# Two gatings cut in two parts and placed in the last projection of an SSD layer, and its first norm placed one chunk later

## The chip, the cores and the metric

The kernel runs on one core of one Trainium2 chip. The metric is the time of one execution on the device in microseconds (us). All times are of that core; the profile of the kernel before was taken in one further execution.

## The reference, cut to what matters

The program computes one inference step of a two-layer decoder trunk for a prompt of 1024 rows and 8 sample rows, 1032 in all (T), at a width of 1024. Layer 0 joins an SSD branch (16 heads) and a convolution branch; both are gated, laid side by side and projected back to the width. Then come the residual and a layer norm. Layer 1 is sparse attention. The change is in the end of layer 0:

```python
y = y.reshape(b, l, SSD_INNER) * jax.nn.silu(z_a)               # gate of the SSD branch
y = y.reshape(b, l, SSD_GROUPS, SSD_INNER // SSD_GROUPS)        # 2 groups of 512 channels
y = y * lax.rsqrt(jnp.mean(jnp.square(y), -1, keepdims=True) + EPS)
y_a = y.reshape(b, l, SSD_INNER) * norm_g
...
out = jnp.concatenate([y_a, y_b], axis=-1) @ w_out              # w_out: 2048 x 1024
x_new = layer_norm(ALPHA * x + out, ln_g, ln_b)
```

## The kernel before, in words

Channels lie on the 128 partitions and rows along the free dimension, so a width of 1024 is 8 tiles of 128 x 1032. Rows are worked on in three chunks of 344: `CH = [(0, 344), (344, 344), (688, 344)]`; below they are the first, second and third chunk. Products keep float32 accuracy by splitting each operand in a high and a low part; `mm3` makes three matrix products for each tile of 128 input channels (lines 132 to 134). One output tile of 128 channels over one chunk is thus 8 x 3 = 24 products, and a chunk of the whole projection is 8 x 24 = 192.

The SSD branch leaves its heads in `xs[0..7]`. Channel tiles 4 to 7 are group 1, tiles 0 to 3 are group 0. `gate(g, t0, n)` does one group on one chunk: for each of its four tiles a load of the saved SiLU of z (`dza`, line 707), a multiplication on VectorE (line 708), a square on ScalarE (line 709) and, from the second tile on, an addition to the running sum (line 711). A product with a matrix of 1/512 (line 714) sums over the partitions; it is f32 and shows as two instructions. ScalarE makes 1/sqrt of it in two steps (lines 174 and 175), each with its table load, and VectorE scales the four tiles (line 718). Four of the six gatings stand among the eight tiles `out_b(m)` of the other branch's projection. The last two, group 0 on the second and third chunk, stand later, before the last projection.

`halves` splits `xs` into the high and low parts `ya` that the projection reads (line 778 on ScalarE, 779 on VectorE or GpSimd). `weights(h, ms)` loads half h of the weights of output tile m (line 763), casts the high part (764) and subtracts for the low part (765, odd m on GpSimd). `rows` loads a chunk's partial results (line 800) into the tiles `part`: two pools, `parts0` for the first and third chunk and `parts1` for the second.

The last loop runs over the three chunks. In the first, the upper four input tiles (kts 4 to 7) of output tiles m = 0 to 6 come first, 12 products each, then the lower four, with the tile added to `part` by line 825; m = 7 is last. The later chunks do 24 products for each m and add by line 830. The results stand in PSUM, in tiles of tag `pp` (two buffers; even m in the later chunks) or `pt` (five buffers, odd m). Behind each chunk stands `layer_norm`: a sum over the eight tiles (line 844), two products for the mean (846 and 847), the subtraction (851), squares (853) and their sum (857), a product for the variance (861), 1/sqrt (174 and 175), scaling (867), the parts for the next layer (868 and 869), the shift (870) and two stores to `dx1` (line 832), issued on GpSimd's queue. The tiles p and q of the norm are of tag `pt`.

The order on each engine is not the order of the program. The build puts the instructions in order by a simulated clock (`schedule_with_timeline_sim=True`): of those that are ready by that clock, the one that stands first in the program goes first. At run time each engine works its queue strictly in that order. Tiles of one tag share the tag's buffers, and the pools `gz`, `ob` and the heads' pool `ssd` give their place to later pools; here `parts1` lies where `gz` lay.

Of the kernel before, what the change touches and what calls it, by code (L numbers as in the profile page):

```python
# [9 lines left out]
F32 = mybir.dt.float32  # L10
# [8 lines left out]
T = 1032  # L19
NP = 1024  # L20
NS = 8
CH = [(0, 344), (344, 344), (688, 344)]
# [62 lines left out]
def psum(k, shape, tag, bufs, dt=F32):  # L85
    return k.t(k.ps, shape, dt, tag, bufs)


def pp(k):
    return psum(k, [128, 344], "pp", 2)  # L90


def pt(k):
    return k.t(k.pb, [128, 512], F32, "pt", 5)


def pm(k):
    return psum(k, [128, 512], "pm", 1)
# [19 lines left out]
def wk(w, kt, m=128, halves=2):  # L118
    per = 8 // halves
    hi, lo = w[kt // per]  # L120
    o = (kt % per) * m
    return hi[:, o : o + m], lo[:, o : o + m]


def mm3(k, out, w, act, t0, n, m=128, halves=2, kts=range(8), start=True, stop=True):

    nc = k.nc
    for kt in kts:
        wh, wl = wk(w, kt, m, halves)
        ah, al = act[kt]  # L130
        ah, al = ah[:, t0 : t0 + n], al[:, t0 : t0 + n]
        nc.tensor.matmul(out, wh, ah, start=(start and kt == kts[0]), stop=False)  # L132
        nc.tensor.matmul(out, wh, al, start=False, stop=False)  # L133
        last = nc.tensor.matmul(out, wl, ah, start=False, stop=(stop and kt == kts[-1]))  # L134
    return last.ins
# [35 lines left out]
def rstd_chunk(k, out, var):  # L171

    nc = k.nc
    nc.scalar.activation(out, var, AF.Ln, bias=k.epsb, scale=1.0)
    nc.scalar.activation(out, out, AF.Exp, scale=-0.5)


def layer0(k):
    nc, A, tc, ctx = k.nc, k.A, k.tc, k.ctx
# [202 lines left out]
    for t0, n in CH:  # L382
        p = pt(k)[:, :n]
# [11 lines left out]
    for t0, n in CH:  # L395
        p = pt(k)[:, :n]
# [75 lines left out]
    gzp = ob_es.enter_context(k.pool("gz"))  # L472
# [6 lines left out]
    for t0, n in CH:  # L479
        p = pp(k)  # L480
        mm_stacked(k, p[:32, :], wdt, x, t0, n)
        nc.scalar.activation(dtr[:32, t0 : t0 + n], p[:32, :], AF.Identity, bias=c("dtb")[:32], scale=1.0)
    p = pm(k)
# [28 lines left out]
    p = pm(k)  # L512
# [13 lines left out]
    for hf in range(2):  # L526
        p = pm(k)
# [3 lines left out]
        sl = slice(hf * 512, hf * 512 + 512)  # L531
# [3 lines left out]
    p = pm(k)  # L535
# [4 lines left out]
    p = pm(k)  # L540
    for hh in range(8):
        for q in range(2):
            h = 2 * hh + q
# [154 lines left out]
    nc.sync.dma_start(A["ssdconv_p"], scp)  # L698


    def gate(g, t0, n):
        sl = slice(t0, t0 + n)
        ob = lambda: k.t(gzp, [128, 344], F32, "gz", 7)
        sm = None
        for i in range(4 * g, 4 * g + 4):
            z = ob()
            nc.sync.dma_start(z, dza[i][:, sl])
            nc.vector.tensor_tensor(xs[i][:, sl], xs[i][:, sl], z, op=ALU.mult)
            nc.scalar.activation(z, xs[i][:, sl], AF.Square)
            if sm is not None:  # L710
                nc.vector.tensor_tensor(z, z, sm, op=ALU.add)
            sm = z
        p = pm(k)[:, :n]
        nc.tensor.matmul(p, k.ones["o512"], sm, start=True, stop=True)
        rs = ob()
        rstd_chunk(k, rs, p)
        for i in range(4 * g, 4 * g + 4):
            nc.vector.scalar_tensor_tensor(xs[i][:, sl], xs[i][:, sl], c("ng")[:, i : i + 1], rs, op0=ALU.mult, op1=ALU.mult)
# [9 lines left out]
    def out_b(m):  # L728
        w = load_w(k, A["W"][OB + m], eng=nc.gpsimd)
        ps = []  # L730
        if m == 7:
            ps = [pp(k), pp(k), pt(k)[:, :344]]
            for p, (t0, n) in zip(ps, CH):
                mm3(k, p, w, yb, t0, n, kts=range(4), stop=False)
        for t0, n in CH:
            o = k.t(obp, [128, 344], F32, "ob", 4)
            nc.sync.dma_start(o, A["xT"][:, m, t0 : t0 + n])
            p = ps.pop(0) if ps else pp(k)
            mm = mm3(k, p, w, yb, t0, n, kts=range(4 * (m == 7), 8), start=m < 7)
            if t0 == 344:  # L740
                four_pages(mm)
            nc.vector.scalar_tensor_tensor(o, o, ALPHA, p, op0=ALU.mult, op1=ALU.add)
            nc.sync.dma_start(dpart[m][:, t0 : t0 + n], o)

    for m in range(8):
        out_b(m)
        if 1 <= m <= 4:
            gate(1 - (m - 1) // 3, *CH[(m - 1) % 3])

# [5 lines left out]
    def weights(h, ms):  # L757
        for m in ms:
# [14 lines left out]
    ya = {i: (k.t(yh_pool, [128, T], F32R, "yh", 8), k.t(*((yh_pool, [128, T], F32R, "yl", 4) if i > 3 else (Yb, [128, T], F32R, "yb", 4))))  # L773
          for i in (4, 5, 6, 7, 0, 1, 2, 3)}

    def halves(i, t0, n):
        sl = slice(t0, t0 + n)
        nc.scalar.copy(ya[i][0][:, sl], xs[i][:, sl])
        (nc.gpsimd if t0 and i % 2 else nc.vector).tensor_tensor(
            ya[i][1][:, sl], xs[i][:, sl], ya[i][0][:, sl].bitcast(F32), op=ALU.subtract)  # L780

    for i in range(4, 8):
        halves(i, *CH[0])
    for t0, n in CH[1:]:
        gate(0, t0, n)
    for i in range(4, 8):
        halves(i, 344, T - 344)
    for i in range(4):
# [2 lines left out]
    op = es.enter_context(k.pool("outp0"))  # L791
    parts = [es.enter_context(k.pool(f"parts{j}")) for j in range(2)]

    dx1 = k.t(dram, [8, 128, T], F32, "dx1")

    def rows(sl):

        prs = [k.t(parts[sl.start == 344], [128, 4, 344], F32, "part", 2) for _ in range(2)]
        for h, pr in enumerate(prs):
            nc.sync.dma_start(pr, dpart[4 * h : 4 * h + 4, :, sl].rearrange("m p t -> p m t"))  # L800
        return prs

    prs = rows(slice(0, 344))
    weights(0, range(8))
    weights(1, range(2))


    for t0, n in CH:
        sl = slice(t0, t0 + n)
        if t0:  # L810
            prs = rows(sl)
            for i in range(4):
                halves(i, t0, n)
        part = [prs[m // 4][:, m % 4, :] for m in range(8)]
        if t0 == 0:
            ps = []
            for m in range(8):
                p = pt(k)[:, :n] if m in (1, 3, 4, 5, 6) else pp(k)
                mm3(k, p, [None, first[m]] if m < 2 else W[m], ya, t0, n, kts=(4, 5, 6, 7), stop=False)
                ps.append(p)  # L820
                if m < 6:
                    continue
                for j in range(7) if m == 6 else (7,):
                    mm3(k, ps[j], W[j], ya, t0, n, kts=(0, 1, 2, 3), start=False)
                    nc.vector.tensor_tensor(part[j], part[j], ps[j], op=ALU.add)
        else:
            for m in range(8):
                p = pt(k)[:, :n] if m % 2 else pp(k)
                mm3(k, p, W[m], ya, t0, n)
                nc.vector.tensor_tensor(part[m], part[m], p, op=ALU.add)  # L830
        layer_norm(k, op, part, n, t0 + n == T, lambda m: [a[:, sl] for a in ya[m]],
                   lambda h, prs=prs, sl=sl: nc.gpsimd.dma_start(dx1[4 * h : 4 * h + 4, :, sl].rearrange("m p t -> p m t"), prs[h]))
    es.close()
    r1_es.close()
    k.x1 = ya
# [3 lines left out]
def layer_norm(k, pool, z, n, last, hl, store):  # L839

    nc, c = k.nc, k.c
    s = k.t(pool, [128, 344], F32, "sum", 1)[:, :n]
    for m in range(1, 7):
        nc.vector.tensor_tensor(s, s if m > 1 else z[0], z[m], op=ALU.add)
    p = pt(k)[:, :n]
    nc.tensor.matmul(p, k.ones["o1024"], s, start=True, stop=False)
    nc.tensor.matmul(p, k.ones["o1024"], z[7], start=False, stop=True)
    q = pt(k)[:, :n]
    sm = None
    for m in range(8):  # L850
        nc.vector.tensor_tensor(z[m], z[m], p, op=ALU.subtract)
        sq = k.t(pool, [128, 344], F32, "sq", 3)[:, :n]
        nc.scalar.activation(sq, z[m], AF.Square)
        if last:
            nc.tensor.matmul(q, k.ones["o1024"], sq, start=(m == 0), stop=(m == 7))
        elif m:
            nc.vector.tensor_tensor(sm, sm, sq, op=ALU.add)
        else:
            sm = sq
    if not last:  # L860
        nc.tensor.matmul(q, k.ones["o1024"], sm, start=True, stop=True)
    rs = k.t(pool, [128, 344], F32, "rs", 1)[:, :n]
    rstd_chunk(k, rs, q)
    for m in range(8):
        hi, lo = hl(m)
        g, b = c("lng")[:, m : m + 1], c("lnb")[:, m : m + 1]
        nc.vector.scalar_tensor_tensor(z[m], z[m], g, rs, op0=ALU.mult, op1=ALU.mult)
        nc.scalar.activation(hi, z[m], AF.Identity, bias=b, scale=1.0)
        nc.vector.scalar_tensor_tensor(lo, z[m], b, hi.bitcast(F32), op0=ALU.add, op1=ALU.subtract)
        nc.gpsimd.tensor_scalar(z[m], z[m], b, 1.0, op0=ALU.add, op1=ALU.mult)  # L870
        if m % 4 == 3:
            store(m // 4)
# [1033 lines left out]
def build(tc, A):  # L1906
    with ExitStack() as ctx:
        k = K(tc, A, ctx)
        setup(k)
        layer0(k)  # L1910
        layer1(k)
# [22 lines left out]
```

## Time and profile before

| what | value |
|---|---|
| time before, median of 3 runs | 1652.54 us (1650.47 to 1658.17) |
| the profiled execution | 1655.23 us, its span 1653.4 us |
| mean granted TensorE clock | 0.986 |
| TensorE (PE) busy | 1582.2 us, 96% |
| VectorE (DVE) busy | 1147.5 us, 69% |
| ScalarE (ACT) busy | 863.9 us, 52% |
| GpSimd (POOL) busy | 424.9 us, 26% |
| last projection, first chunk | 797.69 to 834.10 us of the span |
| second chunk | 834.10 to 873.73 us |
| third chunk | 873.73 to 906.04 us |

A row of the trace's timeline begins with the start and the duration in us, then the engine, the line of the kernel and the operation with its output and inputs by tile name; the bracket at its end is the time for which the engine stood idle before and what ended it. Busy times of PE overlap from one instruction to the next; starts are what counts. PEclk is the TensorE clock that was granted, 1.00 being full speed. The engines' queues are in order, SyncE's (SPq, which issues nearly all loads) too.

### The profile page before, as it was taken

The page shows a single profiled execution, that of the slowest core. Times are in us where ns is not written, and L with a number is a line of the kernel's source. Part 1 is how long each engine was busy: PE and PEld are TensorE (multiplying, and loading weights), DVE is VectorE, ACT ScalarE, POOL GpSimd, SP SyncE. Part 2 cuts the span into 40 slices and gives each one's busy share as a digit, 9 for nine tenths or more (in the row PEclk, how much of TensorE's full clock was granted, in tenths as well). Part 3 has the DMA queues.
Part 4 walks back from the last instruction along what each step waited for, and adds up shares of the span by engine and source line. Part 5 has one row for each costly group of instructions (what it writes and reads, how often), then busy time and mean ns, then how long its engine had stood idle before and what let it go on. Part 6 is the DMA issues. An engine that isn't in the chain of part 4 may idle for free. (4 is left out here: it accounts for less than half of the span.)

```text
span 1653.4 us, 28870 instructions
## 1 busy us (share of the span) xinstructions
PE 1582.2 (96%) x10374; PEld 1426.8 (86%) x10374; DVE 1147.5 (69%) x2375; ACT 863.9 (52%) x1959; POOL 424.9 (26%) x752
## 2 busy tenths in 40 slices
PE   7999989989999998999989999999999899999997
PEld 7999989989999997899889899989997577666675
DVE  4788977542356778684867555999998766565674
ACT  5255433562345556353542544578854855556673
POOL 4000000001222224122514301168762511123330
PEclk9999989999999999999999999999999999999999
DMA  7332232336111145443523321132455413322231
GB/s 231 118 111 73 72 102 95 133 122 216 56 33 52 67 135 177 143 130 97 163 89 106 100 87 39 63 106 92 145 168 172 119 45 109 97 76 63 65 94 45
DMA packets 147397, 173.66 MB, mean 105 GB/s; under 512 B 20117, under 2 KB 111597, under 8 KB 146997
## 3 DMA queue, kind: packets, MB, share of 16 engines
q1 hardware_dynamic: 144596, 165.80, 31.9%
q0 software_dynamic: 1216, 4.37, 0.8%
q10 hardware_dynamic: 1440, 1.65, 0.4%
q8 instruction: 81, 1.33, 0.3%
q14 instruction: 64, 0.52, 0.1%
HBM read 124.04 MB, written 49.82 MB: 105 GB/s over the span
## 5 line engine op out<-in xcount | busy, mean ns | idle before, releaser
L132 PE MATMUL pp<-act,whi 128*128 128x344 f32 x1008 | 328.0, 327 | 13.6 <-ACT act L233 8.1
L134 PE MATMUL pp<-act,wlo 128*128 128x344 f32 x1008 | 329.0, 328 | 10.7 <-DVE wlo L109 10.7
L133 PE MATMUL pp<-act,whi 128*128 128x344 f32 x1008 | 328.0, 325 | 0.9 <-POOL act L726 0.8
L132 PEld LDWEIGHTS pp<-act,whi 128*128 128x128 f32 x1008 | 192.8, 192 | 17.2 <-ACT act L233 8.1
L134 PEld LDWEIGHTS pp<-act,wlo 128*128 128x128 f32 x1008 | 193.1, 192 | 13.1 <-DVE wlo L109 11.6
L133 PEld LDWEIGHTS pp<-act,whi 128*128 128x128 f32 x1008 | 193.1, 192 | 3.3 <-POOL act L726 1.1
L109 POOL TENSOR_TENSOR wlo<-wst,whi 128x512 fp32r<-128x512 f32 x86 | 116.6, 1357 | 305.0 <-ACT whi L108 262.1
L108 ACT CAST whi<-wst 128x512 fp32r<-128x512 f32 x150 | 92.2, 618 | 154.2 <-PE pp L133 74.5
L334 DVE SCALAR_TENSOR_TENSOR uv<-uv,cst,uv 128x1024 f32<-128x1024 f32 x120 | 157.8, 1315 | 2.6
L132 PE MATMUL pp<-yh,whi 128*128 128x344 f32 x412 | 132.9, 323 | 1.5 <-ACT ev L1196 1.5
L134 PE MATMUL pp<-yh,wlo 128*128 128x344 f32 x412 | 132.6, 322 | 1.3 <-POOL wlo L109 1.2
L1510 DVE CUSTOM_DVE_ANT_0 P<-lg,w 128x512 f32<-128x512 f32 (+3 forms) x144 | 82.9, 597 | 55.2 <-PE lg L1509 49.8
L1509 PE MATMUL lg<-w,Q 128*128 128x512 f32 (+3 forms) x384 | 102.4, 371 | 6.3 <-DVE nmx L1510 6.0
L1536 PEld LDWEIGHTS tr<-cst,P 128*128 128x128 f32 x576 | 64.6, 141 | 29.0 <-issue 17.8
L1536 PE MATMUL tr<-cst,P 128*128 128x128 f32 x576 | 85.2, 281 | 4.1 <-ACT P L1514 3.4
L109 DVE TENSOR_TENSOR wlo<-wst,whi 128x512 fp32r<-128x512 f32 x64 | 43.8, 692 | 63.6 <-ACT whi L108 63.2
L1509 PEld LDWEIGHTS lg<-w,Q 128*128 128x128 f32 x384 | 62.8, 191 | 25.6 <-DVE nmx L1510 13.3
L1545 PE MATMUL pv<-ph,V 128*64 128x256 f32 (+1 forms) x640 | 82.6, 375 | 2.0 <-DVE ph L1539 0.9
L134 PEld LDWEIGHTS pp<-yh,wlo 128*128 128x128 f32 x412 | 77.4, 188 | 3.9 <-POOL wlo L109 2.4
L132 PEld LDWEIGHTS pp<-yh,whi 128*128 128x128 f32 x412 | 77.4, 188 | 3.7 <-ACT ev L1196 1.8
L1514 ACT ACTIVATE P<-P,mx 128x1024 f32<-128x1024 f32 (+3 forms) x64 | 63.3, 989 | 30.1 <-DVE mx L1513 27.2
L351 ACT ACTIVATE cft<-cw,own 128x80 f32<-128x80 f32 x256 | 66.2, 349 | 20.8 <-PE pt L353 12.2
(634 smaller groups left out, 4023.3 us busy)
## 6 DMA issues: line engine op xcount, KB each, us to landing
wst<-in_W SPq DMA_DIRECT2D x166, 256.0 KB, 2.9
qst<-dq SPq DMA_DIRECT2D x64, 128.0 KB, 2.8
q<-in_ck SPq DMA_DIRECT2D x64, 128.0 KB, 2.3
vp<-in_cv SPq DMA_DIRECT2D x64, 128.0 KB, 2.1
xst<-in_xT SPq DMA_DIRECT2D x8, 516.0 KB, 9.8
dzb<-ob SPq DMA_DIRECT2D x24, 172.0 KB, 1.9
uv<-dzb SPq DMA_DIRECT2D x8, 516.0 KB, 4.5
dza<-ob SPq DMA_DIRECT2D x24, 172.0 KB, 2.1
```

The lines of the kernel that those rows point to most:

```text
L108: nc.scalar.copy(hi, st)
L109: (eng or nc.vector).tensor_tensor(lo, st, hi.bitcast(F32), op=ALU.subtract)
L132: nc.tensor.matmul(out, wh, ah, start=(start and kt == kts[0]), stop=False)
L133: nc.tensor.matmul(out, wh, al, start=False, stop=False)
L134: last = nc.tensor.matmul(out, wl, ah, start=False, stop=(stop and kt == kts[-1]))
L334: nc.vector.scalar_tensor_tensor(out, x, w[:, j : j + 1], y, op0=ALU.mult, op1=ALU.add)
L351: nc.scalar.activation(wv[:, :, :, ch, :], taps2, AF.Copy, scale=own[:, ch : ch + 1])
L1509: mm = nc.tensor.matmul(lg, Q[:, 4 * a + r, :], KT[g][:, s0 : s0 + m], start=(a == 0), stop=(a == 1))
L1510: dv = nc.vector.tensor_tensor_reduce(out=P[:, s0 : s0 + m], in0=lg, in1=M[tb][:, s0 : s0 + m], scale=-0.125, scalar=BIG, op0=ALU.add, op1 ...
L1514: nc.scalar.activation(P, P, AF.Exp, bias=mx[:, r : r + 1], scale=-1.0, accum_out=rsum[:, r : r + 1])
L1536: nc.tensor.transpose(p[:, a, r * 128 : r * 128 + 128], Ps[r][:, (sb + a) * 128 : (sb + a) * 128 + 128], k.ident)
L1545: nc.tensor.matmul(pv[64 * u : 64 * u + 64, 256 * pr + c0 : 256 * pr + c1], V[:, sb + a, g * 64 : g * 64 + 64], ph[:, a, c0:c1], start=(sb ...
```

## The change

`gate` becomes a generator with a stop (`yield`) between its sums and its product, and takes the pool of its buffers as an argument. The last two gatings run their first parts where they stood, with buffers from a new pool `gz2`, 7 buffers of 344 columns on the right side, which stays open to the end of the loop. Their second parts (product, 1/sqrt, scaling) stand in the first chunk of the last projection: that of the second chunk's gating behind the 12 upper products of m = 5, that of the third chunk's behind the lower products of tile 0. The norm of the first chunk stands behind m = 2 of the second chunk; the other two stay where they were.

```diff
-    def gate(g, t0, n):
+    def gate(g, t0, n, pool=gzp):
         sl = slice(t0, t0 + n)
-        ob = lambda: k.t(gzp, [128, 344], F32, "gz", 7)
+        ob = lambda: k.t(pool, [128, 344], F32, "gz", 7)
...
             sm = z
+        yield
         p = pm(k)[:, :n]
         nc.tensor.matmul(p, k.ones["o512"], sm, start=True, stop=True)
...
-            gate(1 - (m - 1) // 3, *CH[(m - 1) % 3])
+            for _ in gate(1 - (m - 1) // 3, *CH[(m - 1) % 3]):
+                pass
...
-    for t0, n in CH[1:]:
-        gate(0, t0, n)
+    late_es = ExitStack()
+    gz2 = late_es.enter_context(k.pool("gz2", side="right"))
+    gates = [gate(0, *ch, gz2) for ch in CH[1:]]
+    for g in gates:
+        next(g)
...
+    norm = None
     for t0, n in CH:
...
                 ps.append(p)
+                if m == 5:
+                    next(gates[0], None)
                 if m < 6:
                     continue
                 for j in range(7) if m == 6 else (7,):
                     mm3(k, ps[j], W[j], ya, t0, n, kts=(0, 1, 2, 3), start=False)
+                    if j == 0:
+                        next(gates[1], None)
                     nc.vector.tensor_tensor(part[j], part[j], ps[j], op=ALU.add)
...
                 nc.vector.tensor_tensor(part[m], part[m], p, op=ALU.add)
-        layer_norm(k, op, part, n, t0 + n == T, lambda m: [a[:, sl] for a in ya[m]],
-                   lambda h, prs=prs, sl=sl: nc.gpsimd.dma_start(dx1[4 * h : 4 * h + 4, :, sl].rearrange("m p t -> p m t"), prs[h]))
+                if norm and m == 2:
+                    norm()
+                    norm = None
+
+        def norm(part=part, prs=prs, sl=sl, n=n):
+            layer_norm(k, op, part, n, sl.stop == T, lambda m: [a[:, sl] for a in ya[m]],
+                       lambda h: nc.gpsimd.dma_start(dx1[4 * h : 4 * h + 4, :, sl].rearrange("m p t -> p m t"), prs[h]))
+
+        if t0:
+            norm()
+            norm = None
+    late_es.close()
```

## Rows read from the trace of the kernel before

**Rows 1.** The page, part 1: busy us, share of the span, instructions.

```profile
PE 1582.2 (96%) x10374; PEld 1426.8 (86%) x10374; DVE 1147.5 (69%) x2375; ACT 863.9 (52%) x1959; POOL 424.9 (26%) x752
```

**Rows 2.** PE's waits, 797 to 907 us: total, times, longest.

```profile
PE pt L846 <- DVE sum L844: 5.4, 1, 5.4
PE pm L714 <- DVE gz L711: 2.4, 1, 2.4
PE pt L134 <- POOL act L765: 0.5, 1, 0.5
```

**Rows 3.** Stretches: length, busy of PE, PEld, DVE, ACT, POOL, PEclk, DMA share, GB/s.

```profile
797.69:804.29 6.60, 6.60 (x43) 6.31 (x41) 6.60 (x7) 6.58 (x13) 5.41 (x3) 1.00 0.71 221
797.69:834.10 36.41, 33.46 (x199) 32.49 (x198) 26.34 (x38) 23.66 (x42) 20.88 (x12) 0.95 0.52 163
...
794.00:808.00 14.00, 11.55 (x72) 11.07 (x71) 13.96 (x18) 8.43 (x15) 8.60 (x5) 1.00 0.68 220
...
808.00:812.00 4.00, 4.00 (x18) 4.00 (x17) 2.13 (x6) 3.33 (x7) 0.00 (x0) 0.57 0.72 201
834.10:873.73 39.63, 34.23 (x199) 32.91 (x198) 28.72 (x57) 12.88 (x23) 9.64 (x11) 0.91 0.24 84
841.67:846.50 4.83, 4.83 (x15) 4.16 (x16) 0.46 (x2) 0.00 (x0) 0.00 (x0) 0.58 0.30 111
873.73:906.04 32.31, 32.31 (x202) 31.55 (x201) 22.56 (x46) 12.16 (x21) 8.69 (x11) 1.00 0.29 91
```

**Rows 4.** PE's timeline: the first chunk's norm.

```profile
841.67 1.52 PE L846 MATMUL pt<-sum,o 128*128 128x344 f32 x2 [5.40 <-DVE sum L844]
...
845.56 0.80 PE L847 MATMUL pt<-part,o 128*128 128x344 f32 x2
...
857.86 0.74 PE L861 MATMUL pt<-sq,o 128*128 128x344 f32 x2
```

**Rows 5.** PE's groups, 847 to 857.8 us, one of four.

```profile
L132 PE MATMUL pp<-yh,act 128*128 128x344 f32 x23 | 7.5, 324 | 0.0
```

**Rows 6.** DVE's timeline.

```profile
794.06 1.49 DVE L708 TENSOR_TENSOR ya<-ya,gz 128x344 f32<-128x344 f32 x1
...
795.89 1.78 DVE L779 TENSOR_TENSOR yl<-yb,yh 128x344 fp32r<-128x344 f32 x4
...
805.11 1.57 DVE L711 TENSOR_TENSOR gz<-gz,gz 128x344 f32<-128x344 f32 x1
...
831.49 3.77 DVE L718 SCALAR_TENSOR_TENSOR ya<-ya,cst,gz 128x344 f32<-128x344 f32 x4 [1.11 <-ACT gz L175]
835.17 0.50 DVE L825 TENSOR_TENSOR part<-part,pt 128x344 f32<-128x344 f32 x1
...
846.40 3.47 DVE L851 TENSOR_TENSOR part<-part,pt 128x344 f32<-128x344 f32 x8 [4.37 <-PE pt L847]
...
851.06 3.61 DVE L857 TENSOR_TENSOR sq<-sq,sq 128x344 f32<-128x344 f32 x6
...
878.55 3.47 DVE L851 TENSOR_TENSOR part<-part,pt 128x344 f32<-128x344 f32 x8 [3.15 <-PE pt L847]
881.94 0.50 DVE L830 TENSOR_TENSOR part<-part,pp 128x344 f32<-128x344 f32 x1
```

**Rows 7.** Waits of SyncE's queue, 835 to 900 us: total, times, longest.

```profile
SPq L800 <- DMA dx<-part: 38.4, 2, 34.7
...
SPq L800 <- DVE ya L718: 1.1, 1, 1.1
```

**Rows 8.** SyncE's timeline: the third chunk's residual, two loads.

```profile
874.49 4.47 SPq L800 DMA_DIRECT2D part<-dpart x2
```

**Rows 9.** Line 800 by itself: from issue to landing, six loads.

```profile
DMA to landing us min/median/max: 4.2/4.8/5.8
```

**Rows 10.** GpSimd's timeline beside L711.

```profile
803.27 3.04 POOL L765 TENSOR_TENSOR act<-wst,act 128x512 fp32r<-128x512 f32 x2
```

**Rows 11.** ACT's timeline: the first gating's step behind its product.

```profile
807.62 0.55 ACT L174 ACTIVATE gz<-pm,epsb 128x344 f32<-128x344 f32 x1 [2.71 <-PE pm L714]
```

## The prediction

> **What bounds the kernel now.** I read the page first: TensorE (PE) is busy 1582.2 us, 96% of the span [rows 1], so a microsecond is won only where PE stands still or runs slowly. Then the list of PE's waits over the last projection of layer 0: two large ones, 2.4 us for the gating's sum (L711 before the product L714) and 5.4 us for the norm's sum (L844 before L846), and a small one of 0.5 us for a weight's low part [rows 2]. Third, the table by stage, cut where a chunk of the projection begins. A chunk is 192 products plus a few f32 ones. The third chunk has no such wait: 202 products in 32.31 us, 0.160 us each. The first chunk has 199 in 36.41 us, the second 199 in 39.63 us; at 0.160 us both would take 31.8, so 4.6 us are lost in the first and 7.8 in the second [rows 3]. Both losses have a second half behind the wait: PE comes back at half rate. From 808 to 812 the granted clock is 0.57 and 18 products took 4.0 us (2.9 at the fast rate, 1.1 lost); from 841.67 to 846.50 it is 0.58 and 15 took 4.83 us (2.4 lost) [rows 3]. The levels are 1.2 and 2.4 GHz, and PE had stood still before both stretches.
>
> The fourth view is VectorE's (DVE) order [rows 6]. The first gating's last sum ran only at 805.11, behind splits of layer inputs, and the third chunk's gating scaled its rows (L718) from 831.49 for 3.77 us; behind it in the same queue stood the first chunk's evacuations, the next of them at 835.17. So the second wait too hangs on a gating.
>
> **What paces the chunk after next.** The norm of the first chunk does more than fill time. When it is done, its result is stored, and only then can the third chunk's residual be loaded into the same buffers (L800): SyncE waited 38.4 us for those stores in two waits, the load was issued at 874.49 [rows 7, 8] and such a load takes 4.8 us to land, 4.2 at best [rows 9]. The norm's second product L861 was at 857.86 [rows 4]; the load thus comes 16.6 us behind L861 and lands 20.8 behind it. The third chunk's first evacuation L830 was at 881.94, 24.1 behind L861, after the eight L851 of the next norm [rows 6].
>
> And PE can't go round that wait at will. Between L847 and L861 all its products (four groups, of which one is shown) went into pp, the PSUM tag with two buffers, none into pt [rows 5], though m = 1 stands ahead of m = 2 and 4 in the program. The norm's two sums are pt tiles made ahead of m = 1; I read the rows as: a pt tile isn't handed out before the earlier ones in the program have been. So while a norm's L861 is due, PE has only the even m, and the third even m needs the first one's evacuation.
>
> **The change, part by part.**
>
> *The gatings' product and scaling go later.* Nothing is added: each of the two gatings keeps 4 loads, 4 multiplications (L708), 4 squares, 3 additions (L711), a product of two records, two ACT steps with their table loads, 4 scalings. The first one's product goes behind 72 products of the chunk. PE has issued 43 by the wait [rows 3], so 29 more, 4.6 us, come ahead of it, against 2.4 us of waiting: the wait and its 1.1 us of slow clock go. The other gating's product goes behind 96 products. ScalarE's (ACT) steps move with them: L174 waited 2.71 us for the first product, and the next weight cast stood behind it in ACT's queue [rows 11]; such a wait can come again at the new place. Of the 4.6 us in the first chunk I therefore give back 0.8: 0.5 for the weight's low part [rows 2] and 0.3 for casts behind the two ACT chains. So 3.8, with 0 and 4.6 as ends. Second chunk starts at 834.1 - 3.8 = 830.3.
>
> *The first parts stay early and get a pool of their own.* The four loads and seven DVE steps of the last gating no longer wait for the first one's buffers, so they can come right behind L708 at 794.06. Seven steps at about 0.5 us (eight L851 took 3.47) are 3.5 us; DVE is idle later, so this costs nothing unless it comes ahead of the four splits at 795.89, which PE needs at 797.7 [rows 6]. The third chunk's residual load L800 isn't touched; the second one's no longer waits 1.1 us for L718 [rows 7], and that was not on PE's path. On SyncE's queue the four loads go ahead of weight loads; where one waits there for a buffer, the weights wait too, and that is part of the 0.8. The splits of the scaled rows, GpSimd's odd ones among them, move later with the scalings; they are due only at the second chunk's start.
>
> *The norm goes behind m = 2 of the second chunk.* Before, PE had done 13 products of that chunk when it met L846 (from 834.10 to 836.27, where the wait of 5.40 before 841.67 begins). Now it does 72 (11.5 us): L846 at 830.3 + 11.5 = 841.8, with its sum long ready. The wait of 5.4 and the 2.4 of slow clock go. But L846 was at 841.67 before: the norm is no earlier. L847 follows at once, about 842.5; then, as before (845.56 to 857.86 [rows 4]), some 75 products (12.0 us) until L861: 854.5. The earliest it could be: L851 to the end of the last square sum was 846.40 to 854.67, 8.3 us [rows 6], so 850.9. Against 857.86 L861 is 3.4 us earlier, while PE has 59 products, 9.4 us, more behind it at L846.
>
> *What is late next.* Between L847 and the third chunk's third even m PE has 48 + 48 + 72 products. 75 are used up by L861; 93 remain, 14.9 us, with L861 itself and L846/L847 of the next norm 16.0: PE is through at 870.5. The evacuation that frees its buffer comes between 20.8 us (load lands) and 24.1 us (as before) behind L861; I take 22.1, since the next norm's L851 stand ahead of it but start sooner. That is 876.6, and 0.5 for the step: 877.1. PE stands still for 6.6 us in the third chunk, and pays the slow clock again, 2.4 us. In the trace of before this point was 882.4: 5.3 us earlier, less 2.4, is 2.9 us gained. With the evacuation at 20.8, 4.2; with the whole 4.6 in the first chunk, 0.8 more, 5.0. I take the middle of 2.9 and 5.0: 4.0 us. With no gain in the first chunk it is -0.9; with L861 at its earliest 3.6 us more, 8.6.
>
> The profiled execution took 1655.23 us for a span of 1653.4, 2.7 above the median of 1652.54. From 1655.2 the sum gives 1651.2; from the median, which I forecast, **1648.5 us**, the case's own range 1643.9 to 1653.4. I pass the gain on one to one: at 96% busy PE is what the rest waits for too.
>
> **The rivals.**
>
> *All of it is kept.* If the third chunk's odd products may run while L861 is due, PE has 24 to 72 products, 3.8 to 11.5 us, to cover the 6.6. Then both losses go: 4.6 + 7.8 = 12.4 us, 1640.1. For it: the instruction order is drawn anew at build. Against: rows 5. Chance 0.25.
>
> *The first parts come too early (slower).* If the seven DVE steps land ahead of the four splits at 795.89 and each stretches as L708 (1.49) and L711 (1.57, beside GpSimd's L765) did [rows 6, 10], the chunk starts 7 x 1.5 = 10.5 us late. Second chunk at 829.5 + 10.5 = 840, L861 at 864.3, the freeing step at 886.9 instead of 882.4: 4.5 lost, 2.4 slow clock in the third chunk, 1.1 at the start: 8.0, 1660.5. It decides from 4 us of lateness on: then the gain is gone. For it: DVE is busy for 13.96 of the 14 us from 794 [rows 3]. Against: nothing forces them there, as the splits stand first in the program. Chance 0.1.
>
> The Trainium skill has a rule for these stretched steps (SBUF — State Buffer, Who interferes with whom): a VectorE instruction with two SBUF inputs and a GpSimd one that reads SBUF exclude each other, the later one waits. By it the seven moved steps, with two such inputs each, pay for GpSimd's instructions beside them; the 1.57 us L711 agrees, as GpSimd's two L765 ended at 806.31 and L711 at 806.68.
>
> *The order is redrawn and little moves.* If the norm's or the product's place in PE's order doesn't follow the program, the time stays 1652.5. Chance 0.08.
>
> **How the numbers follow.** The main case has 0.57. A change of under 0.5% (8.3 us) is about what a measurement of this kernel can't tell from none. The main case lies inside it but for its lower end (0.05); with the first rival, faster 0.30; the slower rival straddles its bound, and with other late starts slower is 0.10; same 0.60. The range runs from 1640, the first rival, to 1656: it leaves out the slow rival and tails.
>
> **What would show it.** Right: no PE wait at L714 or L846, the first chunk under 33 us, L861 near 854, and a new PE wait of 4 to 8 us for L830 around 871, with half clock behind it and SyncE's L800 still waiting for the stores. Wrong: no such wait (the first rival), products into pt ahead of L861, or L779 of the first chunk and PE's first product of it later than 798. Behind layer 0 the redrawn order can shift a few microseconds either way, which I can't see from here.

## The result, and the profile after

| kernel | median | runs |
|---|---|---|
| before, on the same chip | 1654.13 us | 7 (1650.47 to 1659.42) |
| after | 1662.14 us | 7 (1660.17 to 1662.91) |

The ratio is 1.0053, 95% interval 1.0039 to 1.0066: slower by half a per cent, 8.0 us between the medians, where I had forecast 4.0 less. 1662.14 lies above the range.

First the page's part 1 (after): PE is no busier than before but by 3 us of 1582 [rows 1]; the span of this execution is 1660.4 us.

```profile
PE 1585.4 (95%) x10374; PEld 1428.9 (86%) x10374; DVE 1152.6 (69%) x2375; ACT 865.0 (52%) x1959; POOL 424.0 (26%) x752
```

PE's waits of after, 795 to 910 us (total, times, longest), which answer to [rows 2]. L715 is the old L714, L766 and L767 a weight's cast and low part (old L764, L765), L840 the old L830, L864, L866 and L881 the norm's old L844, L846 and L861:

```profile
PE pp L132 <- DVE part L840: 6.4, 1, 6.4
PE pt L132 <- ACT act L766: 3.2, 1, 3.2
PE pp L132 <- ACT act L766: 1.2, 1, 1.2
PE pt L866 <- DVE sum L864: 0.8, 1, 0.8
PE pm L715 <- DVE gz L711: 0.2, 1, 0.2
```

The first norm's wait is gone and the gating's is down to 0.2 us, as the change meant (the 0.8 us at L866 are the second chunk's norm, at 876.28). In their place stand a wait of 6.4 us in the third chunk, which I had forecast as 6.6, and 4.4 us of waits for weight casts in the first, for which I had 0.3 (and 0.5 for a low part).

The stages of after, cut as in [rows 3], and pieces of them:

```profile
795.66:835.70 40.04, 35.32 (x198) 33.39 (x197) 31.41 (x45) 23.87 (x44) 19.71 (x13) 0.91 0.55 183
835.70:874.90 39.20, 39.20 (x246) 38.60 (x245) 27.63 (x57) 12.03 (x22) 6.71 (x8) 1.00 0.12 40
874.90:909.20 34.30, 27.11 (x155) 25.88 (x154) 23.66 (x47) 12.14 (x21) 12.81 (x34) 0.90 0.34 113
809.00:814.00 5.00, 3.58 (x16) 2.53 (x16) 0.69 (x1) 3.29 (x4) 1.08 (x1) 1.00 1.05 367
...
820.00:824.00 4.00, 4.00 (x19) 4.00 (x18) 3.65 (x4) 0.76 (x2) 2.58 (x2) 0.61 0.43 147
884.06:888.00 3.94, 3.94 (x14) 3.94 (x15) 3.38 (x7) 2.70 (x5) 0.00 (x0) 0.51 0.58 200
```

The first chunk takes 40.04 us, 3.6 more than before [rows 3]; I had 32.6. The second runs at 0.159 us a product without a gap and takes on part of the third's products; second and third together, 401 products both times, take 73.5 us against 71.9. In 820 to 824 and from 884.06 the granted clock is 0.61 and 0.51, behind PE's waits, as before the change behind the old ones.

Of the 7.0 us between the two spans, 5.2 thus lie in this projection. It began 2.0 us sooner in this execution, and some 3 us are lost far behind it, in layer 1's attention, where all queues hold the same order in both kernels: from its first L1529 to its first L1760 (old L1509 and L1740) 97.8 us, before 94.8. That stretch doesn't go with the time: a run with the norm alone moved (below) takes 97.9 there at a ratio of 1.0008, one with the gatings alone 94.8 at 1.0051. So I don't put it down to the change, and of the 8.0 us between the medians these two profiles place 5.2.

### The profile page after: what moved, and what is told of

Read it like the earlier page. It is cut to its first block, busy times and chain, and to the rows that moved or that the text cites. A ratio compares the mean times of both kernels' runs of the same rounds, so it can differ in the third digit from the quotient of the medians.

```text
span 1660.4 us, 28861 instructions
## 1 busy us (share of the span) xinstructions
PE 1585.4 (95%) x10374; PEld 1428.9 (86%) x10374; DVE 1152.6 (69%) x2375; ACT 865.0 (52%) x1959; POOL 424.0 (26%) x752
## 5 line engine op out<-in xcount | busy, mean ns | idle before, releaser
L108 ACT CAST whi<-wst 128x512 fp32r<-128x512 f32 x150 | 92.3, 618 | 158.4 <-PE pp L133 73.5
L1529 PE MATMUL lg<-w,Q 128*128 128x512 f32 (+3 forms) x384 | 104.1, 376 | 8.6 <-DVE nmx L1530 8.3
L1529 PEld LDWEIGHTS lg<-w,Q 128*128 128x128 f32 x384 | 63.5, 193 | 28.9 <-DVE nmx L1530 16.0
L132 PE MATMUL pt<-act,whi 128*128 128x344 f32 x240 | 76.7, 322 | 0.0
```

The costliest lines, as they stand in the source:

```text
L108: nc.scalar.copy(hi, st)
L1529: mm = nc.tensor.matmul(lg, Q[:, 4 * a + r, :], KT[g][:, s0 : s0 + m], start=(a == 0), stop=(a == 1))
```

## The experiments

Each was timed against the kernel before on the same chip. "First chunk" is from its first product to the second chunk's, in one profiled execution; before has 36.4, after 40.0 us. Kernels in which nothing of the first chunk differs agree there within 0.8 us (35.6 to 36.4 for four of them, 39.7 to 40.0 for three). "pm" is a third PSUM tag, that of the gating's product.

| run | ratio | 95% interval | first chunk |
|---|---|---|---|
| gatings only | 1.0051 | 1.0032 to 1.007 | 39.8 |
| norm only | 1.0008 | 0.9996 to 1.0021 | 36.0 |
| after, variance sum in pm | 0.9984 | 0.9972 to 0.9996 | 39.7 |
| before, variance sum in pm | 1.0004 | 0.9988 to 1.002 | 35.6 |
| norm later and sum in pm | 0.9962 | 0.9946 to 0.9977 | 36.4 |
| after without the 1/sqrt | 1.0035 | 1.0022 to 1.0048 | 38.1 |
| one first part later | 1.0056 | 1.0036 to 1.0077 | 40.2 |
| both of these | 1.0024 | 1.0009 to 1.0038 | 38.1 |
| only the last sum in the new pool | 1.0057 | 1.0036 to 1.0079 | 42.4 |
| after, residual load late | 1.003 | 1.0015 to 1.0046 | 37.8 |
| the new pool only | 1.0044 | 1.0022 to 1.0066 | 40.5 |
| the same, load late (two places) | 1.0046, 1.0028 | 1.0029 to 1.0064, 1.0016 to 1.0041 | 42.5, 40.6 |
| load late, no 1/sqrt | 1.0007 | 0.9994 to 1.002 | 35.6 |
| load late, sum in pm | 0.9969 | 0.9952 to 0.9986 | 37.3 |
| load late, a split on GpSimd | 1.0021 | 1.0006 to 1.0036 | 38.5 |
| all three | 0.9984 | 0.9968 to 1.0 | 38.3 |

### Which part costs the time

**Gatings only**: the kernel after, with every norm behind its own chunk.

```diff
-                if norm and m == 2:
-                    norm()
-                    norm = None
...
-        if t0:
-            norm()
-            norm = None
+        norm()
+        norm = None
```

> Only the gatings are cut and moved; each norm stays behind its own chunk. In the trace after, the three chunks lose 8.4, 0 and 9.5 us against 0.160 us a product; before they lost 4.6, 7.8 and 0. Theory A (the gatings' second parts bring 1/sqrt steps ahead of weight casts on ScalarE, and the displaced norm only moves its wait to the third chunk): the first chunk loses 8.4 as in the changed kernel, the second 6 to 8 as before, the third nothing; 15 us against 12.4, ratio about 1.002. Rival B (the displaced norm is the whole cost, the gatings gain as forecast): the first chunk loses under 1, ratio 0.997 or less.

**Norm only**: the kernel before with the first norm behind m = 2 of the second chunk.

> Only the first norm is moved behind m = 2 of the second chunk; the gatings stay whole and where they were. Theory A: first chunk loses 4.6 as before, second nothing, third 9 to 10 with a wait of about 6.4 us for the evacuation; 14 us against 12.4, ratio about 1.001. Rival B: the same wait, but the time goes to the changed kernel's, ratio 1.004 or more.

The gatings alone give 1.0051, nearly the whole 1.0053; the norm alone gives 1.0008, no change that can be told. So the loss is the gatings' edit. The norm's edit is a swap, as expected: it takes the wait of 5.4 us from the second chunk and puts one of 6.3 into the third. From PE's waits of that run, 795 to 910 us:

```profile
PE pp L132 <- DVE part L831: 6.3, 1, 6.3
```

For the gatings alone both expected ratios (1.002, and 0.997 or less) are missed. Its first chunk loses what the change's does, but the old wait of 5.4 us doesn't come back; two others stand behind the first chunk, one for its evacuations (L835) and, behind the projection, one for a square of the last norm (L871, old L855, which waited 1.3 us before). From PE's waits of that run, 795 to 925 us:

```profile
PE pt L871 <- ACT sq L869: 3.8, 1, 3.8
PE pp L132 <- DVE part L835: 3.4, 2, 3.2
...
```

### The wait in the third chunk

**After, variance sum in pm**: the norm's second sum q is no longer a pt tile.

```diff
-    q = pt(k)[:, :n]
+    q = pm(k)[:, :n]
```

> The changed kernel with the norm's second sum (q) in the PSUM tag pm instead of pt, nothing else. Theory A with the reading that a pt tile isn't handed out before the earlier ones: odd output tiles now run ahead of the norm's variance product, the wait of 6.4 us in the third chunk goes with its slow clock, the first chunk still loses 8.4; ratio about 0.997 against the kernel before. Rival (the third chunk waits for its residual whatever PE has to do): the wait stays above 4 us, ratio about 1.005.

PE's waits of this run over the last projection, 795 to 910 us:

```profile
PE pt L132 <- ACT act L766: 1.8, 1, 1.8
PE pp L132 <- ACT act L766: 1.6, 1, 1.6
PE pt L866 <- DVE sum L864: 0.4, 1, 0.4
...
```

The wait of 6.4 is gone (what isn't shown are two waits of 0.2), and PE's list has products into pt between L867 and L881. So the tag held the odd m back, as I had read [rows 5]; the ratio falls by 0.0069, 11 us. The waits for casts in the first chunk stay (3.4 us), and so does its length.

**The same line in the kernel before**, and **in the kernel before with the norm later**:

> The kernel before with the norm's second sum in the PSUM tag pm and nothing else. If the norm's later place is what gains once the third chunk's wait is gone (with both it was 0.9962): the wait of 5.4 us for the norm's sum and the slow clock behind it stay, ratio 0.998 to 1.001. If the free pt tiles alone gain it: 0.995 to 0.997.

> The kernel before with the first norm behind m = 2 of the second chunk and the norm's second sum in the tag pm; gatings as before. Theory: the first chunk loses 4.6 as before, the second and third 0 to 1 (no wait at L846, none for the evacuation); 5 to 6 us lost against 12.4, ratio 0.996. Rival (no more than q in pm gave with the changed gatings, 1.0053 to 0.9984): the first chunk differs by 3.8, so 0.994 at best; if the third chunk still waits for its residual, 0.999 or more.

The line alone gives 1.0004, and PE still waits for the first norm's sum (795 to 910 us):

```profile
PE pt L846 <- DVE sum L844: 3.9, 1, 3.9
```

The norm's place alone gives 1.0008, the two together 0.9962: each takes away the wait that the other would have run into. This version, without the gatings' edit, has the lowest ratio of all that were run, though one of 0.9969 (below) can't be told from it. PE's waits in it, 795 to 910 us, are the old gating's and little else:

```profile
PE pm L714 <- DVE gz L711: 2.5, 1, 2.5
PE pt L134 <- POOL act L765: 0.5, 1, 0.5
PE pt L855 <- DVE sum L853: 0.4, 1, 0.4
```

### The first chunk: ScalarE's 1/sqrt

ScalarE's timeline of after, around the first cast that PE waits for:

```profile
810.67 0.62 ACT L766 CAST act<-wst 128x512 fp32r<-128x512 f32 x1 [3.68 <-DMA wst<-in_W]
811.30 1.28 ACT L174 ACT_TABLE_LOAD   x1
812.60 0.55 ACT L174 ACTIVATE gz<-pm,epsb 128x344 f32<-128x344 f32 x1
813.16 1.28 ACT L175 ACT_TABLE_LOAD   x1
814.46 0.49 ACT L175 ACTIVATE gz<-gz 128x344 f32<-128x344 f32 x1
815.59 0.96 ACT L780 CAST yh<-ya 128x344 fp32r<-128x344 f32 x2 [0.64 <-DVE ya L719]
816.46 0.61 ACT L766 CAST act<-wst 128x512 fp32r<-128x512 f32 x1
```

Two things are seen. The cast at 810.67 waited 3.68 us for its weight to land. And the next cast, at 816.46, stood behind the gating's 1/sqrt, 3.65 us with its two table loads, and a cast that waited for the scaled rows. Each became an experiment.

**After without the 1/sqrt** of the two late gatings:

```diff
-        rstd_chunk(k, rs, p)
+        if pool is gzp:
+            rstd_chunk(k, rs, p)
+        else:
+            nc.scalar.copy(rs, p)
```

> The changed kernel with the 1/sqrt of the two late gatings left out: ScalarE copies the sum instead, one step without a table load in place of two steps with two loads. The output is not the reference's. Theory A: the weight casts no longer queue behind 3.6 us of ScalarE, PE's waits for casts in the first chunk (1.2 and 3.2 us) and the slow clock behind them go for the most part; the first chunk loses 1 to 4 instead of 8.4, the third 9.5 as before; ratio 0.999 to 1.002. Rival (the casts are late because their loads land late): the waits stay within 1 us of 4.4, ratio 1.004 or more.

**One first part later** (the third chunk's gating begins behind m = 5), then **both edits**:

```diff
-    for g in gates:
-        next(g)
+    next(gates[0])
...
                 if m == 5:
                     next(gates[0], None)
+                    next(gates[1])
```

> The changed kernel with the first part of the third chunk's gating (4 loads, 4 multiplications, 3 sums) placed later, behind m = 5 of the first chunk; second parts as in the changed kernel. So far the gatings alone gave 1.0051 and the norm alone 1.0008. Theory A (ScalarE's 1/sqrt steps ahead of weight casts are all of it): the first chunk's waits for casts stay near 3.6 to 4.4 us, ratio 1.005. Theory C (VectorE's multiplications stand ahead of the weight splits that free the buffers for the next weight loads): four of eight such steps go, the waits fall to 1 to 3 us, ratio 1.002 to 1.004.

> As the run before, and 1/sqrt of the two late gatings left out as well (ScalarE copies the sum; the output is not the reference's). Leaving it out alone gave 1.0035 against 1.0053 and left 2.9 us of waits for casts. If A and C add up: waits for casts under 1.5 us, the first chunk loses 1 to 4 us, third chunk's wait of 6.3 us as before, ratio 0.999 to 1.001. If A alone: as without the root alone, 1.003 to 1.004.

Without the 1/sqrt the first chunk is 1.9 us shorter (40.0 to 38.1) and, with the later first part, 2.1 (40.2 to 38.1). So the chain is a cost, but 1.0035 is left, and 2.9 us of the 4.4 of waits for casts: between the two expectations. The place of the third chunk's first part is no cost by itself (1.0056), and both edits together, at 1.0024, can't be told from the first alone. The kernel before has these two chains too and was not run without them; its PE waits for no cast in this projection [rows 2].

**Only the last sum and the 1/sqrt in the new pool**, the loads of z in the old one:

```diff
-        ob = lambda: k.t(pool, [128, 344], F32, "gz", 7)
+        ob = lambda p=gzp: k.t(p, [128, 344], F32, "gz", 7 if p is gzp else 4)
...
-                nc.vector.tensor_tensor(z, z, sm, op=ALU.add)
+                s = ob(pool) if i == 4 * g + 3 else z
+                nc.vector.tensor_tensor(s, z, sm, op=ALU.add)
+                z = s
...
-        rs = ob()
+        rs = ob(pool)
```

> The changed kernel with the late gatings' loads in the old pool gz again and only their last sum and 1/sqrt in gz2 (4 buffers). In the trace after, their loads were issued from 790.3 us on, against 782.4 before, because gz2 lies where the heads' tiles lay. Theory C: loads again about 782 to 786, multiplications in VectorE's gap ahead of the last head, the split of m = 4 near the chunk's start again and not 7 us behind it; the first chunk loses 2 to 5 instead of 8.4, ratio 1.000 to 1.003. Theory A: the waits for casts stay near 4 us, ratio 1.005.

The loads went out early again, from 779.95 us, but this took away nothing (1.0057): PE then also waited 1.7 us for splits of layer inputs, and the weight's split came 5.2 us behind the first product, not near it. All the kernels with the new pool so far also had what comes next.

### The first chunk: the residual load that nobody held back

SyncE's timeline of the kernel before, the loads of line 800 between 798 and 838 us:

```profile
800.31 2.14 SPq L800 DMA_DIRECT2D part<-dpart  x2
835.28 0.93 SPq L800 DMA_DIRECT2D part<-dpart  x2
```

and of after, where that line is L805 and a weight load L765:

```profile
803.25 0.33 SPq L765 DMA_DIRECT2D wst<-in_W  x1
803.64 0.98 SPq L805 DMA_DIRECT2D part<-dpart  x2
804.71 0.45 SPq L765 DMA_DIRECT2D wst<-in_W  x1
805.26 1.18 SPq L805 DMA_DIRECT2D part<-dpart  x2
...
807.38 19.91 SPq L765 DMA_DIRECT2D wst<-in_W  x9
```

The second chunk's residual went out at 835.28 before, because its tiles lay on the last gating's buffers. With the gatings in a pool of their own nothing holds it, and it goes out at 805.26, 30 us earlier, among the weights of the first chunk. From 809 to 814 the DMA engines are full, at 1.05 of their time and 367 GB/s; the same stretch of before:

```profile
809.00:814.00 5.00, 5.00 (x27) 5.00 (x26) 4.00 (x9) 4.19 (x10) 1.86 (x1) 0.75 0.83 246
```

The weight loads issued between 796 and 815 us, after (L765) and then before (L763):

```profile
DMA to landing us min/median/max: 2.6/6.1/8.4
DMA to landing us min/median/max: 2.6/3.1/3.4
```

This holds over all the runs: the median is 5.5 to 6.8 us in the eight kernels whose second residual goes out early, and 2.5 to 4.0 in the eleven others.

**After, residual load late**: a copy of one column makes it wait for rows that the second chunk's gating has scaled.

```diff
         for h, pr in enumerate(prs):
+            if sl.start == 344:
+                nc.gpsimd.tensor_copy(pr[:, 0, 0:1], xs[3][:, 344:345])
             nc.sync.dma_start(pr, dpart[4 * h : 4 * h + 4, :, sl].rearrange("m p t -> p m t"))
```

> The kernel after, but the second chunk's residual load waits, by a copy of one column on GpSimd into its tiles, for the scaled rows of the second chunk's gating; so it goes out behind the weight loads of the first chunk and not at its start, as it did in the kernel before by accident of the buffers' place. Rows theory (the early residual load, four transfers of 688 KB in place of two, takes the bandwidth that the weights of the first chunk need): the two waits for weight casts (3.2 and 1.2 us in the kernel after) fall below 1 us in sum, the first chunk takes 34 to 37 us in place of 40.0, and the ratio to the kernel before is 1.001 to 1.003, since the wait of 6.4 us in the third chunk stays. Chain theory (ScalarE's 1/sqrt of the gatings ahead of the casts): the casts still wait 3 us or more and the ratio stays 1.004 to 1.006.

PE's waits of this run, 795 to 910 us:

```profile
PE pp L132 <- DVE part L842: 6.4, 1, 6.4
PE pp L132 <- ACT act L766: 1.9, 1, 1.9
PE pt L868 <- DVE sum L866: 0.8, 1, 0.8
PE pt L134 <- DVE act L767: 0.7, 2, 0.5
PE pt L134 <- POOL act L767: 0.3, 1, 0.3
...
```

The waits for casts fall from 4.4 to 1.9 us, the weights' median landing to 2.9 (the longest still takes 6.6), the first chunk to 37.8; waits for low parts (L767) of 1.2 us come up. The chunk's length and the waits miss what I had put down for the theory (34 to 37, under 1 us); the ratio of 1.003 fits. The load is one cost of two.

**Load late, no 1/sqrt**: both costs taken out.

> The kernel after with the residual load late and the 1/sqrt of the two late gatings replaced by one ScalarE copy each (no table loads; the scaled rows are then not the reference's). With the load late alone the first chunk took 37.8 us and the ratio was 1.003; the 1/sqrt alone took 1.9 us off the first chunk of the kernel after. If the two are separate costs: first chunk 35.5 to 36.5 us, ratio 1.0005 to 1.002. If the 1/sqrt counts only while the weights are late: first chunk 37 to 38 us, ratio 1.0025 to 1.0035.

The first chunk's stage in this run:

```profile
791.75:827.34 35.59, 33.17 (x197) 30.87 (x197) 31.88 (x48) 17.13 (x36) 19.51 (x15) 1.00 0.63 215
```

35.6 us and 1.0007: the costs are separate and add, as the first expectation had it. Each is worth some 2 us of the first chunk and 0.0015 to 0.0032 of the ratio. With both gone the ratio is that of the norm's move alone (1.0008).

**The new pool only**: the kernel before, whole gatings in their old place, their buffers in gz2.

```diff
-        gate(0, t0, n)
+        gate(0, t0, n, gz2)
```

> The kernel before with one part of the change alone: the two later gatings take their buffers from the new pool, but run whole and where they stood, and every norm stands behind its own chunk. Rows theory: the second chunk's residual tiles no longer lie on buffers of the last gating, their load goes out near the first chunk's, and PE waits 2 to 4 us for weights in the first chunk: ratio 1.001 to 1.0035. Chain theory, and any theory by which the later place of the product or of the norm costs the time: nothing of that is changed, so 0.998 to 1.0005; the loads of z that come earlier could only gain.

It is slower, at 1.0044, with nothing moved in the program, and above the range of the theory (1.001 to 1.0035). The second residual goes out at 804.65 here, so the pool's place alone frees it. PE's waits of this run, 795 to 910 us, are new ones (L827 is the first chunk's evacuation, L832 the later ones'):

```profile
PE pp L132 <- DVE part L827: 7.1, 2, 4.4
PE pp L132 <- DVE part L832: 1.4, 2, 1.3
PE pp L132 <- ACT act L764: 1.2, 1, 1.2
...
```

I had expected 2 to 4 us of waits for weights; only 1.2 are that by name. But the wait of 4.4 us, which ended with VectorE's evacuation at 817.20, goes back to a weight too. From ScalarE's and VectorE's timelines:

```profile
810.07 0.62 ACT L764 CAST act<-wst 128x512 fp32r<-128x512 f32 x1 [4.19 <-DMA wst<-in_W]
814.38 2.04 DVE L718 SCALAR_TENSOR_TENSOR ya<-ya,cst,gz 128x344 f32<-128x344 f32 x4 [2.97 <-ACT gz L175]
817.20 0.50 DVE L827 TENSOR_TENSOR part<-part,pp 128x344 f32<-128x344 f32 x1
```

The cast waited 4.19 us for its weight to land, the gating's 1/sqrt stood behind that cast (from 810.71), VectorE's scaling waited for the 1/sqrt, and the evacuation stood behind the scaling.

**The same with the load late**, first held by the second chunk's scaled rows, then by the third's (column 688), as it was before:

> The kernel before with the gatings' new pool, and the second chunk's residual load made late by the same copy of one column. The pool alone was at 1.0044, its first chunk took 40.5 us where the kernel before took 36.4. Rows theory: with the load late the first chunk is back at 36 to 38 us and the ratio at 0.999 to 1.002. If the new pool costs its time in another way (the z loads that come earlier, VectorE's multiplications ahead of weight splits): the first chunk stays at 39.5 us or more and the ratio at 1.003 to 1.0055.

> As the experiment before, but the second chunk's residual load waits for the scaled rows of the third chunk's gating, as it did in the kernel before by the place of its buffers. In the experiment before SyncE held the weight loads back for 6.6 us behind the load that waited; here the load stands behind all weight loads of the projection. Rows theory: no such wait, the first chunk at 36 to 38 us, the ratio 0.999 to 1.002. If the new pool costs its time in another way (earlier z loads, VectorE's order): first chunk 39.5 us or more, ratio 1.003 to 1.0055.

The first put a new wait in: SyncE held the weight loads behind the load that waited for the copy. Waits of SyncE's queue in that run, 800 to 840 us (L804 is the residual's load, L803 the copy):

```profile
SPq L763 <- POOL act L765: 7.6, 4, 2.6
SPq L804 <- POOL part L803: 6.6, 1, 6.6
SPq L763 <- DVE act L765: 5.6, 4, 2.2
```

The second has the load behind all those weights, and still a first chunk of 40.6 us, with 3.3 us of waiting for a low part on GpSimd; 1.0028 can't be told from 1.0044. So in this kernel the early load isn't the whole cost of the pool, and I count that expectation as missed.

**A split on GpSimd**: one weight's low part (upper half of m = 4) ran 6.9 us behind the first product in every kernel above whose gatings load into the new pool, 0.3 before, and the weight load behind it went out 7.6 us behind that product, 1.0 before. VectorE had multiplications of the second chunk's gating ahead of the split; their loads of z came at 790.29 us in after, not at 782.37 as before. The split goes to GpSimd, in the kernel after with the load late:

```diff
-            (nc.gpsimd if m % 2 else nc.vector).tensor_tensor(...)
+            (nc.gpsimd if m % 2 or (h, m) == (1, 4) else nc.vector).tensor_tensor(...)
```

> The kernel after with the late residual load, and one weight's low part (the upper half of m = 4) made on GpSimd and not on VectorE. In the kernel after this split stood on VectorE behind four multiplications of the second chunk's gating and ran 6.9 us behind the first chunk's first product (0.3 in the kernel before), and the load that waits for its buffer went out 7.6 us behind it (1.0 before). If that is what the first chunk still loses with the residual load late (37.8 us, ratio 1.003): the weight load goes out by 5 us behind the first product, the first chunk takes 36 to 37 us, the ratio is 1.001 to 1.0025. If the order on VectorE costs nothing here: first chunk 37.5 us or more, ratio 1.0025 to 1.0035.

The next weight load still went out 7.2 us behind the first product, so the run didn't do what it was to do, and says nothing on VectorE's order. This late weight load is in every kernel with the new pool (6.9 to 7.6 us), and no run took it away: as a cost of its own it stays untested.

**Combinations**, the load late with the sum in pm, and with the split too:

> Both repairs in the kernel after: the late residual load of the experiment before, and the norm's second sum in the PSUM tag pm. Rows theory with the theory of the third chunk's wait: neither the casts nor the evacuation hold PE up for more than 1 us, and the gains add: 0.9984 of the repair in pm alone less 0.002 to 0.003, so 0.9950 to 0.9965. Chain theory: the first chunk still loses, 0.997 to 0.999.

> The kernel after with three repairs: the late residual load, that one split on GpSimd, and the norm's second sum in the PSUM tag pm. The first and third together were at 0.9969. If the split costs time by itself: 0.9945 to 0.996. If not: 0.9965 to 0.9975. The kernel before with the norm one chunk later and its sum in pm was at 0.9962; below 0.9955 the later gatings would be worth something in the end.

0.9969 and 0.9984: the first lies between its two expectations, the second misses both, and neither passes the 0.9962 that came without the gatings' edit.

## Why the prediction was wrong

**The step that failed** is the first chunk's: "Of the 4.6 us in the first chunk I therefore give back 0.8". The wait for the gating's product went (2.4 to 0.2), but the chunk lost 3.6 us more instead of 3.8 less, 7.4 us off. That is the larger part of the 12.0 us between the forecast (4.0 less) and the result (8.0 more); the two later chunks, forecast 0.2 shorter, took 1.6 more, and 2.8 are placed by no profile. Inside the term two sentences failed. "0.3 for casts behind the two ACT chains" was mis-sized: taking the 1/sqrt out gives 1.9 to 2.2 us in three pairs of runs. And of the second residual load I wrote that it "no longer waits 1.1 us for L718 [rows 7], and that was not on PE's path": I read the 1.1 us that the load had waited at the head of the queue and not when it would now go out. It went 30 us earlier and took bandwidth from the weights, 2.2 to 2.5 us in three pairs of runs that hold it late (after, after with the sum in pm, after without the 1/sqrt).

With both taken out the chunk takes 35.6 us, still 3.0 over my 32.6, so most of the expected gain was not there to have: once PE no longer stands at the gating, it meets the weights (1.1 us for a cast and 0.8 for low parts in that run). What makes those weights late stays open: the load that goes out 7.6 us behind the first product and not 1.0 is a candidate, VectorE's order as its reason was argued, and the run meant to test it missed. What the pool costs by itself (1.0044) is likewise explained only in part.

**What held.** L881, the old L861, came at 860.66, 25.0 us behind the second chunk's start, against 24.2 forecast. The residual load went out 16.6 us behind it, as before. These lines of PE, SyncE and VectorE of after show the chain:

```profile
860.66 0.74 PE L881 MATMUL pt<-sq,o 128*128 128x344 f32 x2
```

```profile
877.30 5.79 SPq L805 DMA_DIRECT2D part<-dpart  x2
```

```profile
883.50 0.94 DVE L840 TENSOR_TENSOR part<-part,pp 128x344 f32<-128x344 f32 x2 [1.86 <-DMA part<-dpart]
```

VectorE itself waits for the load to land, at 883.50, 22.8 behind L881 (22.1 forecast), and PE goes on at 884.06 at half clock. So the forecast of this wait was right for its reason: the norm's move alone brings it (6.3 us), and the norm's second sum in pm takes it away.

**The rivals.** "All of it is kept" was right about what would have been needed, odd products while L861 is due, but only the tag pm gives that. "The first parts come too early" had the right direction, and 1660.5 near the 1662.14, by luck: the first products were not late (795.66), and none of the seven steps stood ahead of the four splits. "The order is redrawn" didn't come: L866 stood at 847.05, 11.4 us into the second chunk, as the program has it (11.5 forecast).

## What to carry to other kernels

A pool of its own for some buffers also frees whatever lies on their old place: list the tiles that come to lie there, the loads that these tiles held back, and what runs when those loads now go out. When a wait is taken out, price the next resource that the engine meets, here weights that arrive just in time, and not only the wait. Two edits that each change nothing can be one gain if each removes the wait that the other runs into.

## What the hardware showed that I had not expected

With four transfers of 688 KB under way in place of two, a weight load of 256 KB took 6.1 us to land in the median instead of 3.1.

GpSimd's split of 344 columns took 4.26 us in the run with the pool alone and the load late, beside VectorE's scalings, multiplications and splits, and the next one 0.91. The Trainium skill (SBUF — State Buffer, Who interferes with whom) has the rule that a VectorE instruction with two SBUF inputs and a GpSimd one that reads SBUF exclude each other. These two spans fit that rule, though the profile's spans on GpSimd are rough.
